# Moving a few waiting tasks in the hand-written step order of a two-layer hybrid decoder kernel

## The chip, the cores and the metric

The kernel runs on one core of a Trainium2 chip. The metric is the device time of one execution in microseconds (us), the median of several runs.

## The reference: what is computed

Two layers over one sequence of 512 tokens and 1024 channels, all in float32. Each layer is a half-step feed-forward block (FFN1), a mixer, and a second half-step feed-forward block (FFN2):

```python
for l in range(DEPTH):
    x = x + 0.5 * swiglu(rms_norm(x, ffn1_norm[l]), ffn1_w_up[l], ffn1_w_down[l])
    h = rms_norm(x, mix_norm[l])
    proj = h @ w_in[l]
    ...
    y_sb = y_sb.reshape(b, s, SB_WIDTH) @ w_branch_sb[l]
    ...
    merged = jax.nn.sigmoid(gate_sb) * y_sb + jax.nn.sigmoid(gate_ssm) * y_ssm
    x = x + merged @ w_out[l]
    x = x + 0.5 * swiglu(rms_norm(x, ffn2_norm[l]), ffn2_w_up[l], ffn2_w_down[l])
return rms_norm(x, final_norm)
```

`swiglu` multiplies `silu(gate)` by `up` over 2816 hidden channels. `y_sb` is a stick-breaking attention of 4 heads of 128 channels: scores, softplus, suffix sums of the softplus over the keys, an exp, and a product with the values. `y_ssm` is a Mamba-2 scan of 24 heads with a causal convolution ahead of it and a step size `dt` per head and token.

## The kernel before

**Layout.** Activations lie transposed: 128 partitions are channels, 512 tokens lie along the free axis. A product of weights with activations goes over k blocks of 128 channels (8 for 1024). Each float32 factor is split into a rounded high part and the rest (names that end in hi and lo; for the attention both carry one name, such as `short` or `bT`), and each product of two blocks is three matmuls (`mm3`, L348 to L352): high x high, then the two mixed ones.

**The order of work.** One Python program writes the instructions of all engines in one order, and each engine runs its own instructions in that order; nothing is reordered later. Dense products form the main line. After each three matmuls of 512 columns (one step) `tick` is called, which lets each side task go on by what it has to do in this step. A side task is a Python generator: `yield n` means that it goes on n steps later. `spawn(task, wait, first)` puts a new task at the end of the list, or with `first=True` at its head; within one step the tasks issue in the order of the list. So the place of a task in the list and its `yield` numbers settle where its instructions stand in the queues of TensorE (PE), VectorE (DVE), ScalarE (ACT) and GpSimd (POOL).

**Weights.** A weight unit is 128 x 1024 numbers (tile `wraw`), loaded from DRAM by SyncE's queue up to four units ahead. `convert(i)` splits unit i: ScalarE casts `whi` (L315), two steps later VectorE subtracts `wlo` (L317). `ahead` (L322 and following), called when a unit is taken into use, spawns the conversions of the next two units, always at the head of the list. There are three pairs of `whi` and `wlo` buffers, so a cast also waits until the products of an older unit are over.

**The opening.** The first two units of layer 0 are loaded in small pieces together with x. Afterwards the square of each x block (tile `tl`, ScalarE L546) is added into `acc` on VectorE (L548), and `norm_end` (L550 and following) makes the normalizing factor `rs` out of the sum: a cast (L555), the rest (L557), two matmuls with a constant (L561), three functions on ScalarE (L565 to L567), three operations on VectorE. The products run on inputs that aren't normalized yet (`hhi`, `hlo`, L533 and L535), and results are multiplied by `rs` afterwards (L580).

**Feed-forward blocks.** 22 blocks of 128 hidden channels. Plain blocks (six at the start of layer 0's FFN1, two at the start of layer 1's) make a gate product and an up product, each into a PSUM bank of four (`mm`), with `gate` (L585 and following: multiply by `rs`, Silu, multiply) and `up` as side tasks. All other blocks are made in pairs by `pair_of_blocks` with seven products instead of eight; `activate` in it waits for GpSimd's multiplication (L653), then issues the Silu (L631). Copies out of PSUM stand between (L658, L666, L669); the one at L669 frees the bank `pa`. Pairs 0 and 2 of each FFN2 (which has no plain blocks) are made together at its start; they are called the leading pairs here.

**Attention.** For each head h and key block j (3 has 128 query columns, 2 has 256, 1 has 384, 0 has 512) `scores(j)` issues three matmuls into one of two `pa` banks, three functions on ScalarE (L968 to L970), one operation on VectorE (L972), a causal mask on GpSimd (L935), and the split into high and low (ScalarE L439, VectorE L444) into the tiles `short` (j = 3) or `xs`. `weights(j)` adds the suffix sums by matmuls with constants (L1005 for the later blocks' totals, tiles `short`, `acc`, `y`; L1007 within the block), then takes the exp out of PSUM (ScalarE L1011), masks it and splits it into `dec`, `btok`, `cT`, `bT` for j = 3, 2, 1, 0. When all four are there, the value product (tile `pt`) follows as 12 matmuls, `bT` first. All this runs beside the mixer's projections, the convolution (`conv_block`, ScalarE L1063, three VectorE operations L1066) and `dt_stage` (two matmuls L865 and L866 into `pt`, VectorE L868 and L869, ScalarE L870 and L871 and others).

Of the kernel before, what the change touches and what calls it, by code (L numbers as in the profile page):

```python
# [17 lines left out]
P = 128  # L18
SEQ = 512
NT = SEQ // P  # L20
DM = 1024
KB = DM // P
DEPTH = 2
SBH = 4
# [89 lines left out]
def pairs_from(layer, f):  # L114

    return {(0, 1): 6, (1, 1): 2}.get((layer, f), 0)
# [57 lines left out]
class Builder:  # L174
# [147 lines left out]
    def ahead(self, look=LOOK):  # L322

        last = len(self.keys) - 1
        while len(self.loaded) <= min(self.pos + look, last):
            i = len(self.loaded)
            while len(self.raw) <= i:
                self.fetch(len(self.raw))
            self.loaded.append(None)
            self.spawn(self.convert(i), first=True)  # L330
        while len(self.raw) <= min(self.pos + self.AHEAD, last) and len(self.raw) - len(self.loaded) < 2:
            self.fetch(len(self.raw))
        for i in range(self.summed, min(self.pos + self.LOOK + 1, last) + 1):
            if self.keys[i][-1] in ("s2", "s4") and self.keys[i][-2]:
                self.spawn(self.add(self.keys[i]))
            self.summed = i + 1
# [267 lines left out]
    def pair_of_blocks(self, base, fp, two):  # L604

        nc, half, n = self.nc, SEQ // 2, KB // 2
        a, b = slice(0, half), slice(half, SEQ)
        diff = self.diff  # L610
        chain, ps2 = (self.t(self.pmm, [P, SEQ], "mm") for _ in range(2))
        ps3 = self.t(self.pa, [P, SEQ], "pa")

        def product(ps, part, rhs, cols, start):
            hi, lo = self.unit(*base, part)
            for j in range(2):
                for k in range(n):
                    ks = slice((j * n + k) * P, (j * n + k + 1) * P)
                    self.mm3(ps[:, j * half:(j + 1) * half], (hi[:, ks], lo[:, ks]),
                             [r[:, cols] for r in rhs[k]], start and j + k == 0, k == n - 1, skip_group_check=True)  # L620
                    if k % 2:
                        self.tick()

        def activate(g, c, cols):

            while self.rs is None:
                yield 1
            norm(nc.gpsimd if c is up1 else nc.vector, g, cols)
            yield 4 if c is up1 else 1
            self.tables(False)  # L630
            nc.scalar.activation(g, g, AF.Silu)  # L631
            yield 1
            if c is up1:
                norm(nc.gpsimd, g, cols)
                yield 3
            while not c:
                yield 1
            r = self.t(fp, [P, SEQ], "a")
            nc.vector.scalar_tensor_tensor(r, c[0], -1.0, g, op0=ALU.mult, op1=ALU.mult)
            yield 1  # L640
            r = r.rearrange("p (j t) -> p j t", j=2)
            yield from self.split([t.rearrange("p (j t) -> p j t", j=2)[:, :, cols] for t in two], r)

        def normed_up(c):
            while self.rs is None:
                yield 1
            norm(nc.gpsimd, c, b)
            yield 3
            up2.append(c)

        def norm(eng, r, cols):
            r = r.rearrange("p (j t) -> p j t", j=2)
            eng.tensor_tensor(r, r, self.rs[:, cols].unsqueeze(1).to_broadcast([P, 2, half]), op=ALU.mult)  # L653

        up1, up2 = [], []
        g1, g2 = (self.t(fp, [P, SEQ], "g", bufs=4) for _ in range(2))
        product(chain, "11", self.h[:n], a, True)
        nc.scalar.copy(g1, chain)  # L658
        product(ps2, "12", self.h[n:], a, True)
        nc.vector.tensor_tensor(g1, g1, ps2, op=ALU.add)  # L660
        self.spawn(activate(g1, up1, a))
        yield
        while None in self.diff:
            self.tick()
        product(chain, "s2", diff[n:], b, False)
        nc.scalar.copy(g2, chain)  # L666
        product(ps3, "s1", diff[:n], a, True)
        c = self.t(fp, [P, SEQ], "c", bufs=2)
        nc.scalar.copy(c, ps3)  # L669
        product(chain, "s3", diff[:n], b, False)  # L670
        nc.vector.tensor_tensor(c, chain, c, op=ALU.add)
        self.spawn(normed_up(c))
        product(ps3, "s4", self.h[n:], b, False)
        nc.vector.tensor_tensor(g2, g2, ps3, op=ALU.add)
        self.spawn(activate(g2, up2, b))
        product(chain, "22", diff[n:], a, False)
        up1.append(chain)
# [100 lines left out]
    def ffn(self, layer, f, gain, gain_next):  # L778
        tc = self.tc
        with tc.tile_pool(name=f"act{layer}{f}", bufs=8, reuse_waits="tile") as ap, \  # L780
                tc.tile_pool(name=f"ffn{layer}{f}", bufs=3, reuse_waits="tile") as fp:
            self.gated = {}
            for s, (j0, j1) in enumerate(SLICES):
                act, quads = [], []
                last = s == len(SLICES) - 1
                for j in range(j0, j1):
                    if j % 2 == 0:
                        two = self.pair(ap, ("act", "act"), (P, 2 * SEQ))
                        act += [tuple(t[:, i * SEQ:(i + 1) * SEQ] for t in two) for i in range(2)]
                    if j >= pairs_from(layer, f):  # L790
                        if j % 2 == 0:
                            quads.append(self.pair_of_blocks((layer, f, "pair", j), fp, two))
                            next(quads[-1])
                        if j % 2 == 0 and (j or pairs_from(layer, f)):
                            for quad in quads:
                                for _ in quad:
                                    pass
                            quads = []
                        continue
                    g = self.t(fp, [P, SEQ], "g", bufs=4)  # L800
                    if self.pos == 0:
                        pg, pu = self.opening(gain)
                        self.spawn(self.gate(pg, g))
                        for k in range(KB // 2):
                            self.spawn(self.combine(k, gain), 12 + 14 * k)
                    else:
                        pg = self.product(self.h, layer, f, "gate", j)
                        self.spawn(self.gate(pg, g))
                        pu = self.product(self.h, layer, f, "up", j)
                    self.spawn(self.up(pu, g, fp, act[-2 + j % 2]))  # L810
                n, both = j1 - j0, []
                for m in OUT_ORDER[:2]:
                    both.append((self.t(self.pmm, [P, SEQ], "mm"), self.unit(layer, f, "down", s, m, ahead=m == 0)))
                    self.dense(*both[-1], act, 0, n - 2, stop=False)
                for i, m in enumerate(OUT_ORDER):
                    if last and gain_next is None and i == KB - 3:
                        self.ending((layer, f, "down", s), act, n, fp)
                        break
                    if i < 2:
                        if i:  # L820
                            self.ahead(1)
                        ps = both[i][0]
                        self.dense(*both[i], act, n - 2, n, start=False, base=0)
                    else:
                        ps = self.t(self.pmm, [P, SEQ], "mm")
                        self.dense(ps, self.unit(layer, f, "down", s, m), act, 0, n)
                    if last and i == 0:
                        self.norm_start()
                        self.xd = self.t(self.dr, [KB, P, SEQ], "xd") if f == 1 else None
                        if f == 1:  # L830
                            self.close_t()
                    self.spawn(self.down(ps, m, gain_next, last))
# [105 lines left out]
    def attention(self, h, parts):  # L938
# [18 lines left out]
        def scores(j):  # L957
# [19 lines left out]
            yield from self.split(two, e)  # L977
            if j == NT - 1:
                behind[j - 1] = two
                yield 2  # L980
            elif j:
                while j not in behind:
                    yield 1
# [11 lines left out]
        def weights(j):  # L995
# [22 lines left out]
            ws[j] = two  # L1018

        self.spawn(scores(3), first=True)  # L1020
        yield 1
        self.spawn(scores(2), first=True)
# [13 lines left out]
        self.attention_on = False  # L1036
        while len(ws) < NT or len(self.v) < NT:
            yield 1
        yield 2
        po = self.t(self.ptr, [P, SEQ], "pt")  # L1040
        for j in range(NT):
            self.mm3(po[:, j * P:], [t[:, h * P:(h + 1) * P] for t in self.v[j]], ws[j], j == 0, j == NT - 1,
# [543 lines left out]
```

## Time and profile before

| what | value |
|---|---|
| runs, median of 3 (lowest to highest) | 2567.6 us (2567.21 to 2567.82) |
| the profiled execution's own time | 2567.14 us |
| its span in the trace | 2565.4 us |
| TensorE's mean granted clock | 0.999 |

The span runs from the first to the last recorded instruction; 1.7 us of the profiled execution's time lie around it. In rows of single instructions the columns are: start in us, duration in us, engine, line, operation, output<-inputs by tile name, shape and type, how many instructions the row joins, and in brackets how long the engine was idle just before and what ended that.

### The profile page before, as it was taken

To read this page: it belongs to the slowest core of one execution; us is meant where nothing else is said; L and a number is where in the kernel's file an instruction comes from. 1 tells how busy PE (TensorE), PEld (TensorE's weight loads), DVE (VectorE), ACT (ScalarE), POOL (GpSimd) and SP (SyncE) were. 2 spreads that over 40 slices of the span, in tenths; PEclk is the share of its full clock that TensorE was granted. 3 is DMA by queue.
4 is the path that set the end of the run, shared out by engine and by line. 5 is a ranking of instruction groups with operands and counts; after the bars stand their busy time and mean duration, and the time that the engine had idled before them with its cause. 6 is when DMAs were issued, how large, how long until landed. Compare 5 with 4: busy or idle time off the path is not lost.

```text
span 2565.4 us, 38502 instructions
## 1 busy us (share of the span) xinstructions
PE 2551.3 (99%) x15176; PEld 2291.4 (89%) x15176; DVE 1728.9 (67%) x2257; ACT 1281.3 (50%) x2115; POOL 553.7 (22%) x662
## 2 busy tenths in 40 slices
PE   9999999999999999999999999999999999999998
PEld 8898988888898889899998989888888888999997
DVE  8576875666564488586885858756666644876766
ACT  6343456665554265343653535566655533643434
POOL 0131301043342013131121312011533310222220
PEclk9999999999999999999999999999999999999999
DMA  6455542233333465555464545423333335656452
GB/s 188 135 150 146 133 139 82 93 120 107 102 110 102 140 196 165 164 140 158 114 180 140 157 140 139 132 80 102 117 97 104 114 111 165 188 146 168 141 163 81
DMA packets 106678, 343.14 MB, mean 134 GB/s; under 512 B 12096, under 2 KB 15616, under 8 KB 106496
## 3 DMA queue, kind: packets, MB, share of 16 engines
q1 hardware_dynamic: 93248, 294.93, 35.1%
q0 software_dynamic: 12384, 45.09, 9.9%
q8 instruction: 119, 1.95, 0.3%
q10 hardware_dynamic: 864, 0.64, 0.1%
q14 instruction: 63, 0.52, 0.1%
HBM read 327.94 MB, written 12.68 MB: 133 GB/s over the span
## 4 chain that ended last, share of the span: by engine, by line
PE 94%; DVE 3%; ACT 1%; issue 1%; DMA 0%; POOL 0%; SPq 0%; DVEq 0%; ACTq 0%; POOLq 0%
PE mm L350 26%; PE mm L352 26%; PE mm L351 26%; PE pa L350 3%; PE pa L352 3%; PE pa L351 3%; PE pa L1212 2%; PE pa L1214 1%; DVE wlo L317 1%; PE pt L890 1%; PE pt L1197 1%; PE pt L1195 1%; PE pa L890 0%; ACT whi L315 0%; PE pa L1007 0%
## 5 line engine op out<-in xcount | busy, mean ns | idle before, releaser
L315 ACT CAST whi<-wraw 128x1024 fp32r<-128x1024 f32 (+3 forms) x438 | 433.3, 989 | 655.5 <-PE mm L352 459.9
L317 DVE TENSOR_TENSOR wlo<-wraw,whi 128x1024 fp32r<-128x1024 f32 (+3 forms) x438 | 537.4, 1227 | 298.5 <-ACT whi L315 298.3
L350 PE MATMUL mm<-hhi,whi 128*128 128x512 f32 (+1 forms) x1552 | 548.8, 354 | 0.0
L352 PE MATMUL mm<-hlo,whi 128*128 128x512 f32 (+1 forms) x1552 | 537.8, 347 | 0.6 <-DVE hlo L535 0.6
L351 PE MATMUL mm<-hhi,wlo 128*128 128x512 f32 (+1 forms) x1552 | 536.7, 346 | 1.2 <-DVE wlo L317 1.2
L352 PEld LDWEIGHTS mm<-hlo,whi 128*128 128x128 f32 x1552 | 293.7, 189 | 38.1 <-DVE hlo L535 1.0
L351 PEld LDWEIGHTS mm<-hhi,wlo 128*128 128x128 f32 x1552 | 294.2, 190 | 33.9 <-DVE wlo L317 1.6
L350 PEld LDWEIGHTS mm<-hhi,whi 128*128 128x128 f32 x1552 | 294.2, 190 | 31.8
L653 POOL TENSOR_TENSOR g<-g,rs 128x512 f32<-128x512 f32 x80 | 165.1, 2066 | 552.2 <-DVE g L660 507.1
L350 PE MATMUL mm<-act,whi 128*128 128x512 f32 (+1 forms) x710 | 274.1, 386 | 0.0
L352 PE MATMUL mm<-act,whi 128*128 128x512 f32 (+1 forms) x710 | 273.8, 386 | 0.0
L351 PE MATMUL mm<-act,wlo 128*128 128x512 f32 (+1 forms) x710 | 273.6, 385 | 0.0
L350 PE MATMUL mm<-th,whi 128*128 128x256 f32 x960 | 268.9, 280 | 0.0
L351 PE MATMUL mm<-th,wlo 128*128 128x256 f32 x960 | 267.9, 279 | 0.0
L352 PE MATMUL mm<-tl,whi 128*128 128x256 f32 x960 | 267.8, 279 | 0.0
L317 DVE TENSOR_TENSOR wlo<-s,whi 128x1024 fp32r<-128x1024 f32 x160 | 234.4, 1478 | 38.3 <-ACT whi L315 35.1
L284 POOL DMA_DIRECT2D s<-in_wflat_dram x86 | 75.4, 876 | 622.2 <-DMA s<-in_wflat_dram 553.1
L681 DVE SCALAR_TENSOR_TENSOR x<-mm,x 128x512 f32<-128x512 f32 x93 | 64.1, 690 | 212.0 <-PE mm L352 212.0
L315 ACT CAST whi<-s 128x1024 fp32r<-128x1024 f32 x160 | 167.8, 1049 | 74.8 <-PE mm L352 52.8
L350 PEld LDWEIGHTS mm<-th,whi 128*128 128x128 f32 x960 | 180.5, 188 | 0.0
L352 PEld LDWEIGHTS mm<-tl,whi 128*128 128x128 f32 x960 | 180.4, 188 | 0.0
L351 PEld LDWEIGHTS mm<-th,wlo 128*128 128x128 f32 x960 | 180.0, 187 | 0.0
(305 smaller groups left out, 5119.5 us busy)
## 6 DMA issues: line engine op xcount, KB each, us to landing
wraw<-in_wflat_dram SPq DMA_DIRECT2D x326, 512.0 KB, 3.6
s<-in_wflat_dram POOLq DMA_DIRECT2D x86, 512.0 KB, 7.2
s<-in_wflat_dram SPq DMA_DIRECT2D x82, 512.0 KB, 5.0
wraw<-in_wflat_dram SPq DMA_DIRECT2D x88, 384.0 KB, 3.1
cumb<-cum_d SPq DMA_DIRECT2D x16, 768.0 KB, 4.7
xd<-x SPq DMA_DIRECT2D x16, 256.0 KB, 2.0
wraw<-in_wflat_dram SPq DMA_DIRECT2D x16, 256.0 KB, 3.1
x<-xd SPq DMA_DIRECT2D x16, 256.0 KB, 5.6
```

Source lines behind the costliest of these rows:

```text
L284: self.nc.gpsimd.dma_start(raw, self.stored(key[:-1] + (part,)), accum_op=ALU.add)
L315: nc.scalar.copy(hi[:, :n], raw[:, :n])
L317: nc.vector.tensor_tensor(lo[:, :n], raw[:, :n], hi[:, :n].bitcast(F32), op=ALU.subtract)
L350: mm(ps, a[0], b[0], start=start, stop=False, **kw)
L351: mm(ps, a[1], b[0], start=False, stop=False, **kw)
L352: mm(ps, a[0], b[1], start=False, stop=stop, **kw)
L653: eng.tensor_tensor(r, r, self.rs[:, cols].unsqueeze(1).to_broadcast([P, 2, half]), op=ALU.mult)
L681: self.nc.vector.scalar_tensor_tensor(x, pd, 0.5, x, op0=ALU.mult, op1=ALU.add)
L890: self.nc.tensor.transpose(pt[:, cs], src[:, cs], self.ident)
L1195: nc.tensor.matmul(pc[:, :P], bt[:, span(c)], ct[:, span(c)], start=True, stop=True)
L1197: nc.tensor.matmul(pu, btok[:, c, :], xws[c].rearrange("p h d -> p (h d)"), start=True, stop=True)
L1212: nc.tensor.matmul(py[:, i * HD:(i + 1) * HD], decs[c][:, i, :], xdts[c][:, i, :], start=True, stop=True)
```

## The change

Four edits, with nothing added to or taken from the computation:

1. `ahead`: the conversions that are spawned while the unit in use is the fifth or an earlier one go to the end of the task list, not to its head.
2. `activate`: in pairs 0 and 2 of an FFN2 the Silu of the first half comes six steps after GpSimd's multiplication, not four.
3. Attention: in head 0, `scores(3)` reports itself as done one step later, so that `weights(3)` starts one step later; in heads 0 to 2 the value product waits three steps, not two.
4. A plain first block (only that of FFN1 in layer 1 comes here): gate runs over k = 0 to 6, then up over k = 0 to 6, then gate's k = 7, and up's k = 7. The task `gate` and the next conversions are spawned between the last two.

```diff
-            self.spawn(self.convert(i), first=True)
+            self.spawn(self.convert(i), first=self.pos > 4)
...
-            yield 4 if c is up1 else 1
+            yield (6 if lead else 4) if c is up1 else 1
...
         up1, up2 = [], []
+        lead = not pairs_from(*base[:2]) and base[-1] < 4
...
-                        pg = self.product(self.h, layer, f, "gate", j)
-                        self.spawn(self.gate(pg, g))
-                        pu = self.product(self.h, layer, f, "up", j)
+                        names = [(layer, f, t, j) for t in ("gate", "up")]
+                        one = [(self.t(self.pmm, [P, SEQ], "mm"), self.unit(*names[0]))]
+                        self.dense(*one[0], self.h, 0, KB - (j == 0), stop=j > 0)
+                        if j:
+                            self.spawn(self.gate(one[0][0], g))
+                        one.append((self.t(self.pmm, [P, SEQ], "mm"), self.unit(*names[1], ahead=j > 0)))
+                        self.dense(*one[1], self.h, 0, KB - (j == 0), stop=j > 0)
+                        if j == 0:
+                            self.dense(*one[0], self.h, KB - 1, KB, start=False, base=0)
+                            self.spawn(self.gate(one[0][0], g))
+                            self.ahead(1)
+                            self.dense(*one[1], self.h, KB - 1, KB, start=False, base=0)
+                        pg, pu = one[0][0], one[1][0]
...
                 behind[j - 1] = two
-                yield 2
+                yield 3 if h == 0 else 2
...
-        yield 2
+        yield 3 if h < SBH - 1 else 2
         po = self.t(self.ptr, [P, SEQ], "pt")
```

In the changed kernel the lines after `ahead` keep their numbers up to L655; then they are one higher, and from the plain blocks on eleven higher (L1007 becomes L1018, L1011 becomes L1022, L870 becomes L881).

**The opening.** On ScalarE, right after the pieces of the first two units, the difference reads so (`wraw_283` is unit 3's load, `wraw_285` unit 4's; `tl` are squares):

```order
 L543 ACTIVATE acc_290<-x_86 128x512
 L546 ACTIVATE tl_105<-x_87 128x512
-L315 CAST whi_303<-wraw_285 128x1024
-L315 CAST whi_306<-wraw_283 128x1024
 L546 ACTIVATE tl_106<-x_88 128x512
+L315 CAST whi_305<-wraw_283 128x1024
+L315 CAST whi_308<-wraw_285 128x1024
 L546 ACTIVATE tl_107<-x_89 128x512
 L546 ACTIVATE tl_108<-x_90 128x512
```

The casts stand one square later, and unit 3 before unit 4. On VectorE, at the same place, the subtractions that make `wlo` turn in the same way:

```order
 L548 TENSOR_TENSOR acc_290<-acc_290,tl_105 128x512
 L548 TENSOR_TENSOR acc_290<-acc_290,tl_106 128x512
-L317 TENSOR_TENSOR wlo_304<-wraw_285,whi_303 128x1024
-L317 TENSOR_TENSOR wlo_307<-wraw_283,whi_306 128x1024
 L548 TENSOR_TENSOR acc_290<-acc_290,tl_107 128x512
+L317 TENSOR_TENSOR wlo_306<-wraw_283,whi_305 128x1024
+L317 TENSOR_TENSOR wlo_309<-wraw_285,whi_308 128x1024
 L548 TENSOR_TENSOR acc_290<-acc_290,tl_108 128x512
```

Unit 3's `wlo` is now the first of the two, and a third sum (of `tl_107`, a square that stands behind both casts on ScalarE) is ahead of it.

**Head 0 of layer 0's attention.** On TensorE before (`short_3734` and the two `xs` are high and low parts, one bank `pa` each for `weights(3)` and `weights(2)`; `mm` rows are the main line):

```order
L352 MATMUL mm_3799<-wlo_3662,hhi_3589 128x512
L1007 MATMUL pa_3742<-short_3734,ntri 128x128 x2
L350 MATMUL mm_3810<-whi_3661,hhi_3578 128x512
L351 MATMUL mm_3810<-whi_3661,hlo_3579 128x512
L352 MATMUL mm_3810<-wlo_3662,hhi_3578 128x512
L1005 MATMUL pa_3749<-short_3734,nones 128x128 x2
L1007 MATMUL pa_3749<-xs_3735,ntri 128x256
L1007 MATMUL pa_3749<-xs_3736,ntri 128x256
```

and in the changed kernel:

```order
L352 MATMUL mm_3799<-wlo_3662,hhi_3589 128x512
L350 MATMUL mm_3808<-whi_3661,hhi_3578 128x512
L351 MATMUL mm_3808<-whi_3661,hlo_3579 128x512
L352 MATMUL mm_3808<-wlo_3662,hhi_3578 128x512
L1016 MATMUL pa_3749<-short_3734,nones 128x128 x2
L1018 MATMUL pa_3749<-xs_3735,ntri 128x256
L1018 MATMUL pa_3749<-xs_3736,ntri 128x256
L1018 MATMUL pa_3742<-short_3734,ntri 128x128 x2
```

The two matmuls of `weights(3)` stand one step of the main line later, behind those of `weights(2)`.

**Head 2 of the same attention.** On ScalarE before (L1011 are the exps of `weights(1)` with 384 columns and `weights(0)` with 512; L870 and L871 belong to `dt_stage`; `y` is a suffix sum, `cv` the convolution):

```order
L439 CAST xs_4215<-cumb_3654 128x512
L315 CAST whi_4448<-wraw_4313 128x1024
L439 CAST y_4217<-cumb_3654 128x384
L1063 ACTIVATE cv_4454<-mm_4376,conv_4136 128x512
L1011 ACTIVATE cumb_3654<-pa_4365 128x384
L870 ACTIVATE sq_4399<-pt_4472 128x96
L871 ACTIVATE sq_4399<-pt_4472 128x96
L1011 ACTIVATE cumb_3654<-pa_4385 128x512
L439 CAST cT_4510<-cumb_3654 128x384
L315 CAST whi_4520<-wraw_4377 128x1024
```

and in the changed kernel:

```order
L315 CAST whi_4444<-wraw_4308 128x1024
L439 CAST xs_4222<-cumb_3654 128x512
L1074 ACTIVATE cv_4452<-mm_4371,conv_4135 128x512
L439 CAST y_4224<-cumb_3654 128x384
L881 ACTIVATE sq_4396<-pt_4468 128x96
L882 ACTIVATE sq_4396<-pt_4468 128x96
L1022 ACTIVATE cumb_3654<-pa_4380 128x384
L315 CAST whi_4512<-wraw_4372 128x1024
L1022 ACTIVATE cumb_3654<-pa_4391 128x512
L439 CAST cT_4520<-cumb_3654 128x384
```

The two operations of `dt_stage` (before L870 and L871, now L881 and L882) have come ahead of the first exp, and a weight cast stands between the two exps. In layer 1 the same rows turn in the same way.

## The prediction

> **What bounds the kernel now.** I read the head of the page first, then TensorE's chain of waits, then single matmuls in the timeline.
>
> ```profile
> span 2565.4 us, 38502 instructions
> PE 2551.3 (99%) x15176; PEld 2291.4 (89%) x15176; DVE 1728.9 (67%) x2257; ACT 1281.3 (50%) x2115; POOL 553.7 (22%) x662
> ```
>
> TensorE is busy 2551.3 of 2565.4 us, and no other engine passes 67%. The change takes no matmul away, so it can only win time in which TensorE stands still. The waits of PE list nearly all of it:
>
> ```profile
> PE mm L351 <- DVE wlo L317: 1.2, 1, 1.2
> PE pa L1007 <- DVE short L444: 0.8, 2, 0.4
> PE mm L352 <- DVE hlo L535: 0.6, 1, 0.6
> PE pa L350 <- ACT c L669: 0.3, 1, 0.3
> ```
>
> Columns: what waits and for what, us in total, times, the longest. These idle times understate the loss, because the rows of neighbouring matmuls overlap. What one costs without a wait is read from the distance of starts. From the first to the second of these rows six matmuls of 512 columns are started:
>
> ```profile
> 1283.70 0.39 PE L352 MATMUL mm<-hlo,whi 128*128 128x512 f32 x1
> ...
> 1285.06 0.39 PE L352 MATMUL mm<-hlo,whi 128*128 128x512 f32 x1
> ```
>
> 1.36 / 6 = 0.227 us for 512 columns (0.113 for 256, 0.057 for 128), and one step of three matmuls is 0.68 us. What two starts lie further apart than that is lost.
>
> The Trainium skill, Perfetto Trace Analysis, section Tensor Engine Instruction (MATMUL, LD_WEIGHTS), says that a matmul's end is computed from its size and not observed, so that starts are the better measure. The rows agree (0.39 us of duration at a pitch of 0.227); by the idle column alone the sum below would be 1.2 + 0.6 + 0.8 = 2.6 us.
>
> **Part 1, the opening** (conversions of units up to the fifth go to the end of the task list).
>
> ```profile
> 22.16 0.39 PE L350 MATMUL mm<-hhi,whi 128*128 128x512 f32 x1
> ...
> 24.27 0.40 PE L350 MATMUL mm<-hhi,whi 128*128 128x512 f32 x1
> 18.13 2.00 ACT L315 CAST whi<-wraw 128x1024 fp32r<-128x1024 f32 x2 [2.01 <-DMA wraw<-in_wflat_dram]
> 20.03 3.23 ACT L546 ACTIVATE tl<-x 128x512 f32<-128x512 f32 x6
> 20.69 0.69 DVE L548 TENSOR_TENSOR acc<-acc,tl 128x512 f32<-128x512 f32 x1 [3.76 <-ACT tl L546]
> 21.30 2.35 DVE L317 TENSOR_TENSOR wlo<-wraw,whi 128x1024 fp32r<-128x1024 f32 x2
> ```
>
> Three matmuls take 24.27 - 22.16 = 2.11 instead of 0.68: 1.43 us lost, to the wlo of unit 3. ScalarE takes unit 4's weights first and waits for their load until 18.13; VectorE then works out unit 4's wlo first, and unit 3's is done only at 21.30 + 2.35 = 23.65. Afterwards unit 3 goes first on both engines. What is late next: its wlo now stands behind a third square sum, whose square stands behind both casts. If unit 3's load lands as early as unit 4's at the latest and its cast of 2.00 / 2 = 1.0 us is over by 18.13, unit 4's cast ends at 19.13, the square follows as at 20.03 one cast earlier (19.03), the sum from 19.7, and wlo from 20.3 to 21.5. TensorE needs it at 22.16 + 0.23 = 22.39: no wait, 0.9 us to spare, gain 1.43. If unit 3's load lands as late as unit 4's, all is 1.0 later, wlo ends at 22.5, and 1.3 is gained. The squares after that come as today. I take 1.43 (low 1.2).
>
> **Part 2, the leading pairs** (a wait of 6 steps instead of 4 before a Silu).
>
> ```profile
> 961.45 0.28 PE L352 MATMUL mm<-tl,whi 128*128 128x256 f32 x1
> ...
> 961.98 0.28 PE L351 MATMUL pa<-hhi,wlo 128*128 128x256 f32 x1
> 2232.31 0.28 PE L352 MATMUL mm<-tl,whi 128*128 128x256 f32 x1
> ...
> 2233.15 0.28 PE L351 MATMUL pa<-hhi,wlo 128*128 128x256 f32 x1
> 2231.77 0.63 ACT L631 ACTIVATE g<-g 128x512 f32<-128x512 f32 x1 [0.58 <-POOL g L653]
> 2232.30 0.57 ACT L669 COPY c<-pa 128x512 f32<-128x512 f32 x1
> ```
>
> Over the 0.23 of two matmuls, 0.30 and 0.61 us are lost here, since the copy that frees the bank pa stands behind the Silu on ScalarE, which waits for GpSimd. The two steps more don't carry the Silu past the copy: no row of any engine changes its place at either spot. Gain 0.
>
> **Part 3, the attention** (the first sums of head 0, and the value products of heads 0 to 2, one step later).
>
> ```profile
> 390.45 0.22 PE L1007 MATMUL pa<-short,ntri 128*128 128x128 f32 x1
> 391.05 0.33 PE L1007 MATMUL pa<-short,ntri 128*128 128x128 f32 x1 [0.38 <-DVE short L444]
> 391.21 0.45 PE L350 MATMUL mm<-whi,hhi 128*128 128x512 f32 x1
> 390.71 0.28 DVE L444 TENSOR_TENSOR short<-cumb,short 128x128 fp32r<-128x128 f32 x1
> 390.91 0.42 DVE L444 TENSOR_TENSOR xs<-cumb,xs 128x256 fp32r<-128x256 f32 x1
> ```
>
> Two matmuls of 128 columns take 0.76 instead of 0.11: 0.65 lost, and the view of waits counts the same stall twice, once a layer. Moved by one step of 0.68, they find short done (390.99). Now the sums of the next block come first, and their last operand xs is done at 390.91 + 0.42 = 391.33, where TensorE wants it at 390.45 + 0.68 + 0.11 + 0.11 = 391.35: between no wait and 0.1 us. I take 0.55 per layer (0.5 to 0.65).
>
> ```profile
> 468.56 0.40 PE L351 MATMUL pt<-bT,yt 128*128 128x512 f32 x1
> ...
> 469.37 0.34 PE L350 MATMUL pt<-cT,yt 128*128 128x384 f32 x1
> 1739.71 0.40 PE L351 MATMUL pt<-bT,yt 128*128 128x512 f32 x1
> ...
> 1740.52 0.34 PE L350 MATMUL pt<-cT,yt 128*128 128x384 f32 x1
> 468.19 0.79 DVE L444 TENSOR_TENSOR bT<-cumb,bT 128x512 fp32r<-128x512 f32 x1
> ```
>
> Two matmuls take 0.81 instead of 0.45, in both layers: 0.36 lost to the low part of bT, done at 468.98 where 468.79 was wanted. One step later it is wanted at 469.48. Gain 0.36 per layer, all of it unless bT itself moves by over 0.5 us.
>
> The price of this part lies in head 2, where the order on ScalarE shown above turns:
>
> ```profile
> 464.09 0.26 DVE L869 TENSOR_TENSOR sq<-pt,sq 128x96 f32<-128x96 f32 x1
> 460.62 0.49 ACT L1011 ACTIVATE cumb<-pa 128x384 f32<-128x384 f32 x1
> 464.38 0.25 ACT L870 ACTIVATE sq<-pt 128x96 f32<-128x96 f32 x1 [3.27 <-DVE sq L869]
> 464.66 0.60 ACT L1011 ACTIVATE cumb<-pa 128x512 f32<-128x512 f32 x1
> 464.05 0.22 PE L350 MATMUL pa<-yt,yt 128*128 128x128 f32 x1
> ```
>
> L870 waits 3.27 us for VectorE's L869. The exp of 384 columns ran 4 us ahead of it; now it is queued behind L870 and L871. The next head's first scores (PE at 464.05) need the bank that this exp reads. If VectorE's chain ends as before (464.35), the exp starts at about 464.66 and ends at 465.15: TensorE waits 1.1 us per layer. But the chain should end earlier: the weight unit's end and the rows of the dt stage lie a step (0.68 us) sooner on TensorE, and the chain, whose last row shows no wait ahead of it, follows by 0.7 to 1.0. That puts the exp's end at 464.15 to 464.45 and the wait at 0.1 to 0.4; I take 0.2 (0 to 1.1). The exp of 512 columns then follows a weight cast; its bank is wanted 1.8 us after the scores, and the cast takes 1.0 and the exp 0.6, so it just holds.
>
> In strict order only this is a wait at all. The Trainium skill, Perfetto Trace Analysis, section Tensor Engine Instruction (MATMUL, LD_WEIGHTS), calls ScalarE and VectorE strict FIFO; the 464.66 row agrees, right behind L871. An engine that picked ready work would make this price 0 and the sum 0.4 larger.
>
> Net per layer 0.55 + 0.36 - 0.2 = 0.71 (-0.25 to 1.0).
>
> **Part 4, the plain first block of layer 1** (seven steps of up before gate's last).
>
> ```profile
> 1286.19 0.39 PE L351 MATMUL mm<-hhi,wlo 128*128 128x512 f32 x1
> ...
> 1287.51 0.39 PE L350 MATMUL mm<-hhi,whi 128*128 128x512 f32 x1
> 1286.38 0.74 DVE L535 SCALAR_TENSOR_TENSOR hlo<-x,par,hhi 128x512 fp32r<-128x512 f32 x1
> 1288.33 1.05 ACT L315 CAST whi<-wraw 128x1024 fp32r<-128x1024 f32 x1
> 1291.59 0.69 ACT L565 ACTIVATE rs<-pt,small 128x512 f32<-128x512 f32 x1 [1.18 <-PE pt L561]
> ```
>
> 1.32 instead of 0.45: 0.87 lost, until hlo of the last norm block is done at 1287.12. Seven steps (4.8 us) of up cover that wholly. The next cast (1288.33) needs gate's weights free, and gate now ends at 1287.51 - 0.87 + 4.8 = 1291.4; L565 stands behind that cast and starts near 1292.6 instead of 1291.59. The norm's factor comes some 1.0 us later; it frees the gate's bank, of which there are four, and I see none wanted so soon. Gain 0.87 (0.7 to 0.87).
>
> **The sum.** 1.43 + 0 + 2 x 0.71 + 0.87 = 3.7 us. The profiled execution took 2567.14 us, 1.7 over its span and 0.5 under the median of the three runs, 2567.6. So the span becomes 2561.7, the profiled execution 2563.4, and the median 2563.9. A measurement of this kernel can tell about 0.2% from no change: 5.1 us, so 2562.5 and 2572.7 are the bounds of "same".
>
> **The rivals.**
> - The exp behind L870 costs 0.6 to 1.1 us per layer, because VectorE's chain doesn't move up. For it: L869's row shows no wait, so the chain itself can't shrink. Against it: what starts it is released a step earlier. Gain 3.7 - 0.8 to 3.7 - 1.8: 2564.7 to 2565.7. Chance 0.20.
> - Part 1 or part 4 doesn't pay in full: wlo of unit 3 waits behind the square sum, or the late L565 holds a bank, 0.5 to 1.4 us. Against it: 0.9 us to spare in the one, four banks in the other. 2564.4 to 2565.3. Chance 0.10.
> - All stalls go, those of the leading pairs too, and the exp costs nothing: 1.43 + 0.91 + 1.3 + 0.72 + 0.87 = 5.2 gives 2562.4. For it: the edit aims at these pairs. Against it: the rows there are the same. Chance 0.05.
> - Slower than before, on the other side: L869 ends late, because a wlo (1.2 us) now stands ahead of y and of the chain to it on VectorE, and that wlo's load or buffer is late. TensorE waits for as long in each layer. 3.7 + 0.4 = 4.1 us of gain are eaten when it waits 2.05 us per layer, that is when L869 ends 1.0 us later than today; at 2 us later the price is 2 x 3.05 and the time 2569.6; over 0.2% slower needs 4.6 us of wait. For it: this queue has no slack. Against it: the list of PE's waits holds no wait for such a load today. Chance 0.05, of which 0.03 beyond 2572.7.
>
> **How the numbers follow.** The forecast has 0.60, and its own range, by the bounds of the parts without the rivals, is 2563.2 to 2564.6. The range that holds 8 in 10 takes in the first two rivals and half the third, and 0.6 us above for the spread of single runs (2567.21 to 2567.82): 2562.5 to 2566.3. Faster by over 0.2% is the third rival and the forecast's far edge, 0.06; slower 0.03; same 0.91.
>
> **What would show it.** In the trace after: the start distances at the five spots fall to the pitch, except at the leading pairs, where 0.3 and 0.6 stay; the wait for wlo in the opening is gone and wlo of unit 3 ends near 21.5; a new wait of PE on the exp (L1022 in the new numbering) at head 2 shows 0.1 to 0.4 in each layer. I am wrong if that wait exceeds 1 us, if the leading pairs' stalls go, or if a wait shows up at a place not named here.

## The result and the profile after

The changed kernel takes 2564.34 us (median of 22 runs, 2563.83 to 2565.38), the kernel before on the same chips 2567.81 us (22 runs): 3.47 us less, a ratio of 0.9986 with a 95% interval of 0.998 to 0.9992. 2563.9 had been forecast. The page's head after, span and busy times:

```profile
span 2562.1 us, 38497 instructions
PE 2549.7 (100%) x15176; PEld 2291.3 (89%) x15176; DVE 1727.9 (67%) x2257; ACT 1279.9 (50%) x2115; POOL 552.4 (22%) x662
```

TensorE does the same 15176 matmuls and bounds the kernel as before. What changed is its list of waits (what waits for what, us in total, times, the longest):

```profile
PE pa L350 <- ACT cumb L1022: 1.3, 2, 0.6
PE pt L1475 <- DVE ones L505: 1.1, 1, 1.1
PE pa L350 <- ACT c L670: 0.3, 1, 0.3
PE pt L729 <- ACT g L717: 0.2, 1, 0.2
```

The waits for wlo, short and hlo are gone, the one for the copy c is still there, and a new one has come twice, on the exp L1022 (L1011 before). The second and fourth row, at the very start and at the last norm, stood in the list before with the same times. Of the runs reported here one, of experiment 1's eleven, took 5876 us; the ratio there leaves it out. The spots of the prediction in turn, first the opening (TensorE, then ScalarE and VectorE):

```profile
22.18 0.39 PE L350 MATMUL mm<-hhi,whi 128*128 128x512 f32 x1
...
22.86 0.39 PE L350 MATMUL mm<-hhi,whi 128*128 128x512 f32 x1
16.73 1.05 ACT L315 CAST whi<-wraw 128x1024 fp32r<-128x1024 f32 x1
18.38 1.05 ACT L315 CAST whi<-wraw 128x1024 fp32r<-128x1024 f32 x1 [0.61 <-DMA wraw<-in_wflat_dram]
20.00 0.69 DVE L548 TENSOR_TENSOR acc<-acc,tl 128x512 f32<-128x512 f32 x1 [2.09 <-ACT tl L546]
20.61 2.36 DVE L317 TENSOR_TENSOR wlo<-wraw,whi 128x1024 fp32r<-128x1024 f32 x2
```

Three matmuls take 0.68, the pitch, where they took 2.11. Unit 3 is cast at 16.73, while unit 4 is still on its way, and its wlo is done at 20.61 + 1.2 = 21.8. The forecast was 21.5; TensorE needs it at 22.40.

Head 0 of layer 0's attention, the sums of both key blocks on TensorE:

```profile
389.64 0.33 PE L1016 MATMUL pa<-short,nones 128*128 128x128 f32 x2
389.81 0.48 PE L1018 MATMUL pa<-xs,ntri 128*128 128x256 f32 x2
390.13 0.33 PE L1018 MATMUL pa<-short,ntri 128*128 128x128 f32 x2
390.30 0.44 PE L350 MATMUL mm<-whi,hhi 128*128 128x512 f32 x1
```

All six take 0.66 us; by the pitch they would take 0.45. Nothing waits for short any more, and the two matmuls with xs take 0.32 for 0.23: xs costs the 0.1 at most that was allowed for it.

Head 2, where the new wait is (VectorE, ScalarE, then TensorE):

```profile
462.35 0.26 DVE L880 TENSOR_TENSOR sq<-pt,sq 128x96 f32<-128x96 f32 x1
462.65 0.25 ACT L881 ACTIVATE sq<-pt 128x96 f32<-128x96 f32 x1 [4.38 <-DVE sq L880]
462.92 0.50 ACT L1022 ACTIVATE cumb<-pa 128x384 f32<-128x384 f32 x1
462.45 0.40 PE L352 MATMUL mm<-hlo,whi 128*128 128x512 f32 x1
463.47 0.33 PE L350 MATMUL pa<-yt,yt 128*128 128x128 f32 x1 [0.63 <-ACT cumb L1022]
```

The exp ends at 463.42, and TensorE goes on at 463.47. From 462.45 to 463.47 is 1.02 for one matmul of 0.23: 0.80 us lost (0.81 in layer 1). The value product of the same head, and the leading pair, by their first and last start:

```profile
468.45 0.39 PE L350 MATMUL pt<-bT,yt 128*128 128x512 f32 x1
...
469.13 0.33 PE L350 MATMUL pt<-cT,yt 128*128 128x384 f32 x1
...
959.64 0.28 PE L352 MATMUL mm<-tl,whi 128*128 128x256 f32 x1
...
960.17 0.28 PE L351 MATMUL pa<-hhi,wlo 128*128 128x256 f32 x1
```

Three matmuls with bT take 0.68: that stall is gone. At the leading pair two matmuls take 0.53 where 0.23 is the pitch: its 0.30 is still there (and 0.60 in layer 1). Last, layer 1's plain first block:

```profile
1281.67 0.39 PE L351 MATMUL mm<-hhi,wlo 128*128 128x512 f32 x1
...
1288.25 0.39 PE L561 MATMUL pt<-rs,nones 128*128 128x512 f32 x1
1290.36 1.05 ACT L315 CAST whi<-wraw 128x1024 fp32r<-128x1024 f32 x1 [1.87 <-PE mm L352]
1291.32 0.68 ACT L565 ACTIVATE rs<-pt,small 128x512 f32<-128x512 f32 x1
```

29 matmuls in 6.58 us, 0.227 each: no stall. The cast waits for gate's end and L565 stands behind it, as forecast, though later than worked out (below).

Where the time came from, by the start of the matmul with the same number in both traces (before less after, read at places where both traces do the same work):

| up to (us, before) | gain so far | what lies between |
|---|---|---|
| 22 | 0.0 | start |
| 60 | 1.48 | the opening |
| 395 | 2.06 | head 0: +0.58 |
| 1280 | 1.80 | rest of layer 0's attention: -0.26 |
| 1300 | 2.58 | the plain first block: +0.78 |
| 1664 | 3.17 | layer 1, head 0: +0.59 |
| 1900 | 2.94 | rest of layer 1's attention: -0.23 |
| last matmul | 2.87 | leading pairs and the rest: -0.07 |

From the last matmul's start to the end of the span it is 10.13 us before and 9.69 after, another 0.44. 2.87 + 0.44 = 3.31, the difference of the two profiled executions (2567.14 and 2563.83). Of the attention's later rows, 0.36 gained at bT less 0.80 lost at the exp would be -0.44; the table has -0.26 and -0.23, so some 0.2 per layer was gained that no term held.

### The profile page after: what moved, and what is told of

Read it like the earlier page. It is cut to its first block, busy times and chain, and to the rows that moved or that the text cites. A ratio compares the mean times of both kernels' runs of the same rounds, so it can differ in the third digit from the quotient of the medians.

```text
span 2562.1 us, 38497 instructions
## 1 busy us (share of the span) xinstructions
PE 2549.7 (100%) x15176; PEld 2291.3 (89%) x15176; DVE 1727.9 (67%) x2257; ACT 1279.9 (50%) x2115; POOL 552.4 (22%) x662
## 4 chain that ended last, share of the span: by engine, by line
PE 98%; DVE 1%; ACT 1%; issue 0%; POOL 0%; DMA 0%; SPq 0%; DVEq 0%; ACTq 0%; POOLq 0%
PE mm L350 27%; PE mm L352 27%; PE mm L351 27%; PE pa L350 3%; PE pa L352 3%; PE pa L351 3%; PE pa L1223 2%; PE pa L1225 1%; PE pt L1208 1%; PE pt L901 1%; PE pt L1206 1%; PE pa L489 0%; PE pa L901 0%; PE pa L1018 0%; PE pt L352 0%
```

## The experiments

The gains in the next table are the median of the kernel before, measured beside each kernel on the same chip, less that kernel's median (11 runs, the changed kernel 22). Their intervals are wide against the effects (0.0009 of the time is 2.3 us), so the verdicts rest on the starts in the traces, one execution of each kernel, and the medians beside them.

| kernel | us | less than before by | ratio, 95% interval |
|---|---|---|---|
| changed kernel | 2564.34 | 3.47 | 0.9986 (0.998 to 0.9992) |
| 1 first sums alone | 2565.85 | 1.83 | 0.9993 (0.9984 to 1.0002) |
| 2 leading pairs alone | 2567.63 | 0.05 | 0.9999 (0.999 to 1.0008) |
| 3 changed, dt exps 3 steps later | 2562.37 | 5.31 | 0.9979 (0.9971 to 0.9988) |
| 4 changed, Silu after 7 steps | 2564.92 | 2.76 | 0.9988 (0.998 to 0.9997) |
| 5 value products alone | 2567.29 | 0.67 | 0.9996 (0.9987 to 1.0005) |
| 6 changed without first sums | 2564.67 | 3.29 | 0.9986 (0.9978 to 0.9995) |
| 7 opening in order, at the head | 2566.95 | 1.01 | 0.9996 (0.9987 to 1.0005) |
| 8 changed, dt exps 1 step later | 2562.77 | 5.19 | 0.998 (0.9971 to 0.9989) |
| 9 as 3, second pair on VectorE | 2563.69 | 4.01 | 0.9984 (0.9975 to 0.9993) |
| 10 as 3 without first sums | 2564.51 | 3.19 | 0.9987 (0.9978 to 0.9996) |
| 11 as 3 without later value products | 2563.40 | 4.30 | 0.9983 (0.9974 to 0.9992) |
| 12 plain first block alone | 2566.60 | 1.10 | 0.9995 (0.9987 to 1.0004) |

The theory: all terms as forecast, but the exp behind L881 costs 0.8 us per layer. The rival: the exp is late whatever stands ahead of it.

**3. The dt stage's exps later.** In `dt_stage` of the changed kernel:

```diff
         nc.vector.tensor_tensor(left, pt[:, n:2 * n], cum, op=ALU.subtract)
+        yield 3
         nc.scalar.activation(grown, pt[:, :n], AF.Exp)
         nc.scalar.activation(ecb, pt[:, n:2 * n], AF.Exp)
```

> The changed kernel, in which the two exps of the dt stage (L881, L882) are issued three steps later, so that they stand behind both exps of head 2 on ScalarE. Theory (the exp of 384 columns waits only because L881 stands ahead of it): the waits on L1022 go, 0.8 us by starts in each layer, 1.6 us faster than the changed kernel, about 5.0 us faster than before. Rival (the exp or its operands are late anyway, since ScalarE and VectorE are behind in head 2): the waits stay at 0.4 us or more, the gain is under 0.8 us.

Head 2 of layer 0 in its trace (L1023 is the exp, L882 the first exp of the dt stage):

```profile
460.87 0.49 ACT L1023 ACTIVATE cumb<-pa 128x384 f32<-128x384 f32 x1 [1.76 <-DVE y L444]
463.01 1.05 ACT L315 CAST whi<-wraw 128x1024 fp32r<-128x1024 f32 x1 [1.65 <-PE mm L352]
463.96 0.59 ACT L1023 ACTIVATE cumb<-pa 128x512 f32<-128x512 f32 x1
464.45 0.50 ACT L439 CAST cT<-cumb 128x384 fp32r<-128x384 f32 x1
464.86 0.25 ACT L882 ACTIVATE sq<-pt 128x96 f32<-128x96 f32 x1
463.28 0.40 PE L352 MATMUL mm<-hlo,whi 128*128 128x512 f32 x1
463.51 0.22 PE L350 MATMUL pa<-yt,yt 128*128 128x128 f32 x1
```

The exp runs at 460.87, two us before it is wanted, and the scores follow the main line at the pitch (0.23). By starts 0.79 and 0.82 come back in the two layers, 1.6 together, as the theory said; the rival is out. Against before the median gains 5.31 us where the changed kernel gains 3.47. This is the lowest median of the study; experiment 8 is too close to it for the medians to part them.

**8. One step later only.** The same edit with `yield 1`: the exps of the dt stage then stand between the two exps of head 2.

> The changed kernel, with the two exps of the dt stage one step later: behind the exp of 384 columns, but ahead of a weight cast and the exp of 512. Theory (each bank waits for what stands ahead of its exp): the wait of the next head's scores(3) goes; scores(2) waits 0.1 to 0.3 us for the exp of 512; 1.0 to 1.4 us faster than the changed kernel. Rival (the cost is the two exps of the dt stage themselves, wherever they stand in head 2): the 0.8 us per layer stays, now at scores(2).

```profile
463.34 0.22 PE L350 MATMUL pa<-yt,yt 128*128 128x128 f32 x1
465.20 0.39 PE L350 MATMUL pa<-yt,yt 128*128 128x256 f32 x1
464.54 0.61 ACT L1023 ACTIVATE cumb<-pa 128x512 f32<-128x512 f32 x1
```

scores(3) at 463.34 don't wait. The exp of 512 ends at 465.15, and scores(2) start at 465.20, right behind it: a wait of about 0.1, too short for the list of waits. 0.7 per layer comes back. The cost belongs to the place in ScalarE's queue and not to the two instructions. The Trainium skill, Perfetto Trace Analysis, section Tensor Engine Instruction (MATMUL, LD_WEIGHTS), has ScalarE as strict FIFO; experiments 3 and 8 agree, with 0.8 and 0.7 us per layer for a place in the queue.

**1. The first sums alone.** The kernel before with one edit:

```diff
-                yield 2
+                yield 3 if h == 0 else 2
```

> The kernel before with the edit of head 0's first sums alone. Theory (this edit is what brings L870 and L871 ahead of the first exp of head 2): the stall of 0.65 us in head 0 falls by 0.55 in each layer, and a wait of TensorE on the exp of 384 columns at head 2 appears, 0.6 us in the view of waits and 0.8 by starts, in each layer. Sum: 2 x (0.8 - 0.55) = 0.5 us slower than before. Rival (the wait on the exp comes from the value products' later start, or from the late chain on VectorE and not from the place in ScalarE's queue): no wait on the exp, 1.1 us faster than before.

The theory fell: no listed wait on the exp, 1.1 us of gain by starts from 60 us on (1.83 in the median). L870 does stand ahead of the first exp, but TensorE comes for the bank a step later too. Head 1's value product, and head 3's first scores beside the exp that they wait for:

```profile
440.96 0.50 PE L350 MATMUL pt<-bT,yt 128*128 128x512 f32 x1
...
442.02 0.34 PE L350 MATMUL pt<-cT,yt 128*128 128x384 f32 x1
...
463.71 0.26 DVE L869 TENSOR_TENSOR sq<-pt,sq 128x96 f32<-128x96 f32 x1
464.28 0.50 ACT L1011 ACTIVATE cumb<-pa 128x384 f32<-128x384 f32 x1
464.83 0.33 PE L350 MATMUL pa<-yt,yt 128*128 128x128 f32 x1
```

Three matmuls with bT take 1.06 instead of 0.68. Head 1's weights come a step later by the edit, and the value product now waits 0.38 for bT, where it did not wait before. The exp ends at 464.78, and TensorE goes on at 464.83, 0.31 behind the matmul before: it is held up for 0.08 at most (0.06 in layer 1). The main line is level with the kernel before here (a difference of 0.00), so times compare as they stand: L869 ends at 463.97, 0.38 sooner than before. In the changed kernel it ends 0.32 later than before by the same measure (worked out in the next section). So the wait on the exp there takes both edits: the first sums, which turn ScalarE's queue, and the later value products, without which the main line loses 0.38 at head 1 and the chain ends sooner against it. Experiment 6, with the value products and without the first sums, has no wait on the exp either.

**5. The value products alone.**

```diff
-        yield 2
+        yield 3 if h < SBH - 1 else 2
```

> The kernel before with the later value products (heads 0 to 2) alone. Theory: the stall at head 2's bT goes, 0.36 us by starts in each layer, nothing new, since the order of the exps on ScalarE stays: 0.7 us faster than before. Rival (the value product a step later pushes what follows into a wait, as the first sums did in the first experiment at head 1's value product): no gain or a loss, with a new stall of 0.2 us or more within two us of a value product.

0.67 us faster, and in the trace 0.67 from 60 us on: as the theory said, with no new stall in the attention.

**6. The changed kernel without the first sums.** The line of experiment 1 taken back.

> The changed kernel without the edit of head 0's first sums. Theory (in the changed kernel this edit takes 0.58 us of stall away in head 0 and brings 0.8 us at head 2's exp, in each layer): the waits on L1022 go, those for short come back, 0.4 us faster than the changed kernel, 3.9 us faster than before. Rival (the first sums are worth what they gained alone, 1.1 us in the trace up to the last matmul and 1.8 in the median): 1.1 to 1.8 us slower than the changed kernel.

Neither came. By starts from 60 us on it equals the changed kernel (a difference of 0.00 at the last matmul): the waits for short are back, the waits on the exp are gone, and 0.2 per layer, which the theory hadn't, makes up the rest. In the changed kernel the edit of the first sums earned nothing on the main line.

**10 and 11. What the two attention edits are worth when the exps are free.** Experiment 3's kernel without the one and without the other.

> The third experiment's kernel without the edit of head 0's first sums. Theory (with the exps freed, the first sums earn their whole 0.58 us per layer): 1.2 us slower than the third experiment, both stalls at short back. Rival (what the sixth experiment measured, that the first sums are worth nothing here): the third experiment's time within 0.3 us.

> The third experiment's kernel without the later value products. Theory (beside the moved first sums the value products of heads 1 and 2 both come too early: 0.4 us at head 1, as in the first experiment, and up to 0.36 at head 2): 0.8 to 1.5 us slower than the third experiment, stalls at bT back. Rival (head 2's bT comes earlier once the exps are free, and head 1's stall belongs to the first experiment's order alone): slower by under 0.4 us.

Without the first sums 2.1 us are lost against experiment 3 (1.6 by starts from 60 us on), without the value products 1.0 (0.9 by starts, 0.4 at each head 1; head 2's bT is in time). Both edits pay there. The first sums bring 0.8 per layer, not 0.58: 0.62 by head 0, the other 0.2 between 470 and 600 us, spread over small matmuls that the traces don't tie to a wait.

**2 and 4. The leading pairs.** First the edit alone on the kernel before, then the changed kernel with `7 if lead` for `6 if lead`, the first number with which the Silu goes behind the copy.

> The kernel before with the edit of the leading pairs alone (6 steps instead of 4). Theory (no instruction changes its place): the time of before within 0.3 us, and the two stalls at the copy c stay, 0.3 and 0.6 us by starts. Rival (the later Silu lets the copy through in time): 0.9 us faster than before.

> The changed kernel, with a wait of 7 steps instead of 6 in the leading pairs, the first number that brings the Silu behind the copy c on ScalarE. Theory (the copy is late only because the Silu ahead of it waits for GpSimd): both stalls go, 0.3 and 0.6 us by starts, 0.9 us faster than the changed kernel, 4.4 us faster than before. Rival (the later Silu makes the rest of the pair late, or the bank is freed late for another reason): the time of the changed kernel, with the stalls in place or a new wait behind them.

Six steps do nothing (0.05 us). Seven steps take the stall at the copy away (a net gain of 0.28 in each layer), and more comes back further on, 0.42 by starts at the next weights, in each layer:

```profile
971.21 0.28 PE L350 MATMUL mm<-th,whi 128*128 128x256 f32 x1
971.70 0.39 PE L351 MATMUL mm<-th,wlo 128*128 128x256 f32 x1 [0.22 <-DVE wlo L317]
```

The rival was right: the kernel is 0.7 us slower than the changed one by the medians' differences, 0.3 by starts.

**9. The second pair's multiplication on VectorE**, in experiment 3's kernel:

```diff
-            norm(nc.gpsimd if c is up1 else nc.vector, g, cols)
+            norm(nc.gpsimd if c is up1 and not (lead and base[-1]) else nc.vector, g, cols)
```

> The third experiment's kernel (the two exps of the dt stage three steps later), in which the multiplication L653 of the second leading pair's first half goes to VectorE (1.1 us) and not to GpSimd (2.2 us, behind the first pair's). Theory (the copy c is late because the second Silu waits for the second of GpSimd's two multiplications): the stalls at c go, 0.3 to 0.6 us in each layer, 0.7 us faster than the third experiment. Rival (the leading pairs have no slack behind them either, as the fourth experiment showed): VectorE's 1.1 us delay a wlo, a stall of 0.2 us or more comes instead, no gain.

```profile
962.05 0.28 PE L352 MATMUL pa<-hlo,whi 128*128 128x256 f32 x1
962.78 0.36 PE L350 MATMUL mm<-th,whi 128*128 128x256 f32 x1 [0.46 <-DVE c L672]
...
959.72 2.32 DVE L317 TENSOR_TENSOR wlo<-wraw,whi 128x1024 fp32r<-128x1024 f32 x1
957.00 3.95 POOL L653 TENSOR_TENSOR g<-g,rs 128x512 f32<-128x512 f32 x2 [0.83 <-ACT g L631]
```

ScalarE's copy no longer holds TensorE up, but VectorE does: 0.41 at a wlo (at 956.48) and 0.62 at c in layer 0, 0.41 and 0.78 in layer 1. By the medians' differences it is 1.3 us slower than experiment 3, by starts 1.0. The rival was right again; its "0.2 us or more" came out at 0.4 to 0.8 at each place.

**7. The opening in order, but at the head of the list.** In `ahead` of the kernel before (`new` counts from 0):

```diff
-            self.spawn(self.convert(i), first=True)
+            self.side.insert(new, [self.convert(i), 0])
+            new += 1
```

> The kernel before, with the opening's conversions still at the head of the task list, but unit 3 ahead of unit 4. Theory (only the order of the two units counts, not their place in the list): the stall of 1.43 us goes, 1.4 us faster than before. Rival (the place behind the square sums counts): the wait for wlo stays at 1 us or more, no gain.

The stall at wlo goes whole (1.46 by starts), so the order of the two units made it. But the place in the list counts too. With one square sum fewer ahead of the conversions, the norm's sum ends later, and its second matmul waits; 0.34 of the gain is lost there, and 1.01 is left in the median:

```profile
28.39 0.39 PE L562 MATMUL pt<-rs,nones 128*128 128x512 f32 x1
28.88 0.50 PE L562 MATMUL pt<-sq,nones 128*128 128x512 f32 x1
```

**12. The plain first block alone.**

> The kernel before with the plain first block's edit alone. Theory: the stall at hlo goes whole, 0.87 us by starts, and the norm's factor, which comes 1 us later, holds nobody up: 0.8 to 0.9 us faster than before. Rival (the later factor holds a bank or a cast): under 0.5 us faster, with a new wait of TensorE between 1287 and 1310 us.

0.89 by starts at 1289 us, 0.81 at 1300 (the norm's matmuls start a little apart), 1.10 in the median; no wait for the later factor.

## Why the prediction was right or wrong

The time and the side were right, in part by luck: one term of the sum was too good by 0.6 us per layer, and two gains that nobody forecast made up for most of it.

- **Part 1, the opening:** forecast 1.43, measured 1.48 by starts. The chain ran as worked out, with wlo at 21.8 for 21.5. The size was read from the one execution that it is compared with; other traces without this edit lose 0.86 to 1.9 at this spot (last section).
- **Part 2, the leading pairs:** forecast 0, measured 0 (experiment 2: 0.05).
- **Part 3, the first sums and bT:** 0.55 and 0.36 per layer forecast; 0.58 in head 0 (0.59 in layer 1), and the stall at bT gone, are measured.
- **Part 3, the exp behind L870:** the step that failed. It was priced at 0.2 per layer, in a range of 0 to 1.1, because "the weight unit's end and the rows of the dt stage lie a step (0.68 us) sooner on TensorE", and the chain would follow by 0.7 to 1.0. It cost 0.80, and 0.6 in the list of waits, where 0.1 to 0.4 was to be seen. The premise misread the rows. In both traces the same 2100 matmuls of the main line (those into `mm`) stand ahead of the dt stage's first matmul, 8028 in layer 1. What moved is the attention, a step down: head 3's first scores stand behind 2112 main-line matmuls before and 2115 after, 8040 and 8043 in layer 1. The dt stage's rows on TensorE and its third function on ScalarE, before:

```profile
460.01 0.36 PE L865 MATMUL pt<-raw,upto 128*128 128x96 f32 x2
455.83 0.27 ACT L854 ACTIVATE sq<-raw 128x96 f32<-128x96 f32 x1
```

and after, with the start of ScalarE's queue and what VectorE does with the function's result:

```profile
457.37 0.35 PE L876 MATMUL pt<-raw,upto 128*128 128x96 f32 x2
446.68 0.48 ACT L1135 COPY z<-mm 128x384 f32<-128x384 f32 x1 [1.82 <-DVE rs L1125]
...
454.10 0.27 ACT L865 ACTIVATE sq<-raw 128x96 f32<-128x96 f32 x1
454.40 0.21 DVE L867 TENSOR_SCALAR raw<-raw 128x96 f32<-128x96 f32 x1 [1.43 <-ACT sq L865]
```

The main line is 2.06 us ahead of the kernel before at this place, so 2.06 is added to compare. The dt matmuls then start at 459.43, 0.58 sooner than 460.01, only because the four matmuls of weights(1) now stand behind them. L865 starts at 456.16, 0.33 later than L854 before. From L867 on VectorE works with no gap shown up to L880, which ends at 462.61 + 2.06 = 464.67, 0.32 later than before and not 0.7 sooner; the exp ends at 463.42 + 2.06 = 465.48. The scores, at the pitch, would start at 462.45 + 0.23 + 2.06 = 464.74, 0.69 later than the 464.05 that the prediction went by. 465.48 - 464.74 = 0.74, and 0.05 from the exp's end to the matmul's start makes the 0.8. Between TensorE and the chain stands ScalarE's queue, which from 446.68 to 458.3 has no gap over 0.5 us in the trace after. That this full queue, late from the copies of z on, is what holds L865 back is read from the trace and wasn't tried.

  The rival named for this (0.6 to 1.1 per layer, 2564.7 to 2565.7) had the reason right, that VectorE's chain doesn't move up, and the size in part by luck: by the prediction's own working such a chain costs 1.1, and the later scores took back more than the chain lost. Its time was not reached because of the last point.
- **Part 4:** forecast 0.87, measured 0.78 to 0.89. Gate's end was put too early: the norm's two matmuls (0.52 us from 1288.25) run ahead of it, and L565 starts 0.5 later than worked out, at 1291.32 + 1.80 = 1293.12 for 1292.6. Nothing waited for it.
- **The sum:** 1.48 + 0.78 and 0.3 per layer instead of 0.71 give 2.9 up to the last matmul, 0.8 short of the forecast 3.7. The exp alone was 1.2 short for both layers; the 0.2 per layer that no term held made up for 0.4 of it. More came from a place taken as untouched, the end of the span: 0.44 in the profiled execution, none of it work of TensorE. The medians' 3.47 holds all of this.

## What to carry to other kernels

Where one engine is busy all the time, the distance of its starts prices each stall well: five of six such terms held within 0.1 us. A moved task's price hides in the queues that it passes: ask which engine paces the chain in front of a waiting instruction. When two rows change places, count on the main line which of them moved: here the chain had kept its step and its neighbours had gone down one. Edits of one schedule don't add: the first sums were worth 1.1 us by starts alone, 0.0 in the changed kernel and 1.6 once the exps stood elsewhere, so test an edit in the company that it will keep.

## What the runs showed of the hardware that was not expected

- From the last matmul's start to the end of the span the traces have one of two values, with one between: 9.68 to 9.70 us (the changed kernel, experiments 1, 3, 8, 9, 11), 10.04 to 10.17 (before, 2, 4, 5, 7, 10, 12) and 9.88 (6). The instructions there are the same in all, and so is the work: 6.51 us after that start the last computing instruction ends, and by 6.89 the last store is issued, in every trace. The values part behind that, in SyncE's last waits (the fifth begins 7.80 us after the start before, 7.57 in the changed kernel). The six short ones all have the edit of the first sums; 4 has it too and is long. Where medians differ by more than the starts, experiments 1, 4, 6 and 10 fit these values and 9 doesn't. Each was seen in one execution, and the cause stays open.
- The opening's loads don't land at the same time in each execution: the matmul that starts at 22.16 us before starts between 22.2 and 23.1 in the other traces, and the stall there without the edit was 0.86 (experiment 12), 1.4 (before and experiment 1), 1.8 (5) or 1.9 us (2).
- VectorE's subtraction for a wlo takes 1.22 us in most rows, but 2.32 in experiment 9, beside GpSimd's multiplication (957.00 to 960.95). No run changed this alone.
